# Hybrid decoder trunk on one core: expert steps of two 512-column blocks, 4 KB weight runs, later rows gathered from split operands

## The chip, the cores and the metric

The kernel runs on one core of one Trainium2 chip. The metric is the device time of one execution in microseconds (us). Before the change it is 1590.65 us, the median of 3 runs (1590.27 to 1591.75).

## What is computed

The reference runs two layers over a float32 residual stream of 256 tokens by 1024 features. Each layer has three token mixers (S5, SSD, gated DeltaNet) between an input and an output projection, and then a feed-forward part: dense SwiGLU in layer 0, and in layer 1 the top 2 of 8 SwiGLU experts, followed by a final RMSNorm. The change touches the experts alone:

```python
def moe_ffn(h, w_router, w_gate, w_up, w_down):
    logits = (h @ w_router).astype(jnp.float32)
    top_v, top_i = lax.top_k(logits, TOP_K)
    top_w = jax.nn.softmax(top_v, axis=-1)
    combine = jnp.sum(jax.nn.one_hot(top_i, N_EXPERTS) * top_w[..., None], axis=-2)
    out = jnp.zeros_like(h)
    for e in range(N_EXPERTS):
        out = out + combine[..., e:e + 1] * swiglu(h, w_gate[e], w_up[e], w_down[e])
    return out
```

`w_gate` and `w_up` are 1024 by 3584 for each expert and `w_down` is 3584 by 1024, all float32. That is 44.04 MB an expert and 352.3 MB for the eight, and every byte is read once.

## The kernel before

`moe` (L1326) does not multiply all 256 tokens by all experts. `route` finds for each token its two experts and its rank among the expert's tokens. From the ranks `one_hot` (L1387) builds 0/1 matrices, and `gather` (L1394) multiplies X by them on TensorE, which picks the rows of one expert into a few columns. Experts 2 to 6 have 64 slots, experts 0 and 1 have 64 and another 32 ("few"), expert 7 has 128 and 32. The rows are gathered in three batches (`BATCHES`, L1317): 64 columns for expert 2, 256 columns for experts 7 and 0, 352 columns for 3, 4, 5, 6 and 1. Batch 0 is gathered ahead of the branch (L1454 to L1455), the other two in pieces called `gap()` between the steps (L1673 to L1683). If any expert has more tokens than slots, a general path is taken (L1797 to L1800); with this data it is the other path, `stream` (L1669).

`stream` walks `STEPS` (L1313): 56 steps, each one expert and one block m of 512 of its 3584 inner columns. Experts 2 and 0 are interleaved first, then expert 7 with 3, 4 and 5, then 1 and 6. A step multiplies the gathered rows by the gate and up block (`half_up` L1522 for 64 slots with a gate and an up product side by side in the array; `few_up` L1530; `split_up` L1495 for expert 7), scales the result out of PSUM on ScalarE (L1735), then does the down product of the step before (`down` L1685, with `half_down`, `few_down`, `split_down`), and then turns its own gate and up result by TensorE transposes (`turn_half` L1558) and applies SiLU and the product (`gated` L1550). float32 matmuls show as two instructions each. Expert 7 alone works in float32r: `staged` (L1487) splits each weight tile into a high and a low part, by a ScalarE copy (L1491) and a VectorE subtraction (L1492), into buffers of which there are three. When an expert is done, `put_back` (L1641) adds its rows to X in two halves. These halves are called one at a time inside the next step's up product (L1729), as `late`.

TensorE's order is the order of the program (`manual_schedule`, L1803); the other engines' order is planned by the framework. PSUM has four banks of tag "G" for everything that is short-lived: up products, transposes, gathers and put-backs.

Weights come through a ring of 14 slots of 1 MB, loaded in the order of use by SyncE's queue. `load_up` (L1331) fills a slot with 256 rows of one gate block and one up block in two DMAs of 512 KB; a row of a block is a run of 2 KB in memory. `load_down` (L1341) fills one with 256 rows of `w_down`, two whole rows or 8 KB for each partition. A slot is loaded again when its last reader on TensorE is done. The first 14 loads are issued ahead of the branch (L1450).

Of the kernel before, what the change touches and what calls it, by code (L numbers as in the profile page):

```python
# [46 lines left out]
def tile_hymba_trunk(ctx: ExitStack, tc: tile.TileContext, p: dict, out: bass.AP):  # L47
# [1264 lines left out]
    BESIDE = [(e, m) for e in (3, 4, 5) for m in range(7)]  # L1312
    STEPS = [(2, 0), (2, 1), (2, 2), (0, 0), (0, 1), (2, 3), (0, 2), (0, 3), (2, 4), (0, 4), (2, 5), (0, 5), (2, 6), (0, 6)]  # L1313
    STEPS += [x for m in range(7) for x in BESIDE[3 * m:3 * m + 1] + [(7, m)] + BESIDE[3 * m + 1:3 * m + 3]]
    STEPS += [(1, 0), (6, 0), (1, 1), (6, 1), (1, 2), (1, 3), (6, 2), (1, 4), (6, 3), (1, 5), (6, 4), (1, 6), (6, 5), (6, 6)]

# [9 lines left out]
    def moe(ring):  # L1326
# [4 lines left out]
        def load_up(e, m, k2):  # L1331
# [23 lines left out]
        def ups(e, m):  # L1355
            return [lambda k2=k2: load_up(e, m, k2) for k2 in range(4)]

        def downs(e, m):
            return [lambda i=i: load_down(e, i) for i in (2 * m, 2 * m + 1)]

        def w_loads(steps):

            out, prev = [], None
            for x in steps:
                out += ups(*x) + (downs(*prev) if prev else [])
                prev = x
            return out + downs(*prev)
# [45 lines left out]
        def take_in(b, on=G, **kw):  # L1413

            c0, c1 = BOUNDS[b]
            oh = act.tile([128, 2, c1 - c0], F32, name="oh", **kw)
# [4 lines left out]
            def step(k):  # L1421
                if k == 7:
                    for e, first in BATCHES[b]:

                        o, n = PLACE[e, first]
                        slot_scale(rsl[:max(64, n), RS[e, first]:RS[e, first] + 1], oh[:, :, o - c0:o - c0 + n])
                px = ps("G", "pxe")[:, :c1 - c0]
                gather(px, k, oh, X)
# [19 lines left out]

        with scope("nrm"):
            ready = [f() for f in w_loads(STEPS)[:len(ring)]]  # L1450
            rest = route(cw, rk, cnt, r)
            todo = take_in(0, V)
            rest()
            for f in todo:  # L1454
                f()  # L1455

        with scope("experts"):
            def back(e, first=0):
# [4 lines left out]
                def rest():  # L1463
                    if e == STEPS[-1][0]:
                        slot_scale(cws, od, cw[:, :, e:e + 1])
                    ots[e, first] = turned(od, tag="ohT", bufs=5)
                return rest

            def more(e, n, x, x0, first=128):
# [3 lines left out]
                for k in range(8):  # L1473
                    px = ps("G", "pxm", (128, n))
                    gather(px, k, oh[:, :, :n], x0)
# [3 lines left out]
                return x, turned(oh, tag="ohT", bufs=5), rs  # L1479

            def wide_up(pgu, x, w, k2):
                for q in range(2):
                    for kk in range(2):
                        k = 2 * k2 + kk
                        T.matmul(pgu[q], lhsT=x[:, k], rhs=w[:, 2 * q + kk, :], start=k == 0, stop=k == 7)
# [8 lines left out]

            def split_up(pgu, w, k2):  # L1495
                for q in range(2):
                    h, l = staged(w[:, 2 * q:2 * q + 2])
# [24 lines left out]
            def half_up(pp, x, w, k2):  # L1522

                for kk in range(2):
                    k = 2 * k2 + kk
                    for q in range(2):
                        T.matmul(pp[64 * q:64 * q + 64], lhsT=x[:, k, :], rhs=w[:, 2 * q + kk, :], start=k == 0, stop=k == 7,  # L1527
                                 tile_position=(0, 64 * q), skip_group_check=True)

            def few_up(pp, x, w, k2):  # L1530

                for j in range(4):
                    T.matmul(pp[32 * j:32 * j + 32], lhsT=x[:, 2 * k2 + j % 2, :], rhs=w[:, j, :], start=k2 == 0, stop=k2 == 3,  # L1533
# [30 lines left out]
            def turn_few(g):  # L1564
# [5 lines left out]
                t = act.tile([128, 8 * FEW], F32, name="tf", tag="tf")  # L1570
# [3 lines left out]
                return gated(t, FEW, "hf")  # L1574
# [35 lines left out]
            def final(src, wF):  # L1610

                ss = act.tile([128, 2, 2], F32, name="ssf")
                for n in range(2):
                    for f in range(2):
                        j = act.tile([128, 512], F32, name="sqj", tag="gsf")
# [53 lines left out]
            def stream(ready):  # L1669
# [3 lines left out]
                two, one = (take_in(b, tag="y", bufs=3) for b in (1, 2))  # L1673
                todo = [lambda i=i: [f() for f in two[i:i + 2]] for i in range(0, 8, 2)] + one
# [6 lines left out]
                def gap():  # L1681
                    if todo:
                        todo.pop(0)()  # L1683

                def down(e, m, hs):  # L1685
                    split_ = GROUPS[e][0][1] == 128
                    if m == 0:
# [6 lines left out]
                    w = [take(), take()]  # L1694
                    for c2 in range(2):
                        (split_down if split_ else half_down)(acc[e][0], hs[0], w[c2], c2, m)
                    if len(hs) > 1:
                        for c2 in range(2):
                            few_down(acc[e][1], hs[1], w[c2], c2, m)
                    if (e, m) == STEPS[-1]:  # L1700
# [8 lines left out]
                    elif m == 6:  # L1709
                        assert not todo  # L1710
                        of = [(a, ots[e, first]) for a, (first, _) in zip(acc[e], GROUPS[e])]
                        late.extend(put_back(e, of[0], of[1:]) if split_ else put_back(e, None, of))

                for e, m in STEPS:
                    split_, few = GROUPS[e][0][1] == 128, len(GROUPS[e]) > 1
                    rs = [rsl[:, RS[e, first]:RS[e, first] + 1] for first, _ in GROUPS[e]]
                    pgu = [ps("G", "pmg") for _ in range(1 + split_)]
                    pgf = ps("G", "pmf") if few else None
                    for k4 in range(2):
                        w = [take(), take()]  # L1720
                        for k2 in range(2):
                            if split_:
                                split_up(pgu, w[k2], 2 * k4 + k2)
                            else:
                                half_up(pgu[0], rows(e, 0), w[k2], 2 * k4 + k2)
                        if few:
                            for k2 in range(2):
                                few_up(pgf, rows(e, GROUPS[e][1][0]), w[k2], 2 * k4 + k2)
                        if late:  # L1729
                            late.pop(0)()  # L1730
                    if split_:
                        g = gate(pgu, rs[0], "gs0")
                    else:
                        g = act.tile([128, 512], F32, name="gs", tag="gs0")
                        A.activation(out=g, in_=pgu[0], func=AF.Identity, scale=rs[0])  # L1735
                    if few:
                        gf = act.tile([128, 512], F32, name="gs", tag="gsf")
                        V.tensor_scalar(out=gf, in0=pgf, scalar1=rs[1], scalar2=None, op0=OP.mult)  # L1738
                    gap()
                    if prev:  # L1740
                        down(*prev)
                    gap()
# [3 lines left out]
                    if 2 <= m < 2 + len(GROUPS[e]):  # L1746
                        turns[e] = back(e, GROUPS[e][m - 2][0])
# [119 lines left out]
```

## Time and profile before

| | us |
|---|---|
| median of 3 runs | 1590.65 (1590.27 to 1591.75) |
| the profiled execution | 1594.89 |
| its span, first to last instruction | 1592.8 |
| before the experts' weights arrive | about 661 |
| expert stage, to the end of the last down product | about 661 to 1579 |

A profile is one execution. Busy TensorE time is the time between a matmul's start and its modelled end, so that a busy engine is not one at its peak; a "granted clock" of 1.00 is 2.4 GHz and 0.50 is 1.2 GHz. A "chain" is found by going back from the last instruction to what released it. "issue" is time in which nothing is seen that the engine waited for. GB/s is what the 16 DMA engines moved.

### The profile page before, as it was taken

The page shows a single profiled execution, that of the slowest core. Times are in us where ns is not written, and L with a number is a line of the kernel's source. Part 1 is how long each engine was busy: PE and PEld are TensorE (multiplying, and loading weights), DVE is VectorE, ACT ScalarE, POOL GpSimd, SP SyncE. Part 2 cuts the span into 40 slices and gives each one's busy share as a digit, 9 for nine tenths or more (in the row PEclk, how much of TensorE's full clock was granted, in tenths as well). Part 3 has the DMA queues.
Part 4 walks back from the last instruction along what each step waited for, and adds up shares of the span by engine and source line. Part 5 has one row for each costly group of instructions (what it writes and reads, how often), then busy time and mean ns, then how long its engine had stood idle before and what let it go on. Part 6 is the DMA issues. An engine that isn't in the chain of part 4 may idle for free.

```text
span 1592.8 us, 23174 instructions
## 1 busy us (share of the span) xinstructions
PE 1510.6 (95%) x9287; PEld 950.9 (60%) x9287; DVE 678.0 (43%) x1344; ACT 481.3 (30%) x817; POOL 156.9 (10%) x278
## 2 busy tenths in 40 slices
PE   4899979999999999889999999999999999999996
PEld 4898959999998999754333344544444444333322
DVE  7898684545567988520010051422422433100102
ACT  4562354454345543321110031321321332000101
POOL 5911081020000100030000000000000000000000
PEclk9999999999999989979999999999999999999998
DMA  6431044555545430399999999999999999999995
GB/s 171 146 105 53 1 149 132 186 182 177 189 156 146 133 107 1 116 360 381 356 348 396 398 395 398 395 398 396 398 396 398 397 397 397 398 397 395 398 397 203
DMA packets 203908, 435.80 MB, mean 274 GB/s; under 512 B 14539, under 2 KB 67876, under 8 KB 189712
## 3 DMA queue, kind: packets, MB, share of 16 engines
q1 hardware_dynamic: 201088, 432.20, 73.7%
q0 software_dynamic: 928, 1.43, 0.4%
q8 instruction: 75, 1.23, 0.3%
q10 hardware_dynamic: 1776, 0.60, 0.1%
q14 instruction: 41, 0.34, 0.1%
HBM read 433.15 MB, written 1.05 MB: 273 GB/s over the span
## 4 chain that ended last, share of the span: by engine, by line
PE 58%; DMA 7%; DVE 2%; ACT 1%; issue 1%; SPq 0%; DVEq 0%; ACTq 0%
PE pmg L1527 19%; PE macc L1587 10%; PE pmf L1533 5%; PE pmg L1501 4%; DMA ringb<-in_moe_w_down_dram 3%; PE maccf L1593 2%; PE macc L1510 2%; PE pmts L1561 2%; PE psc L1651 1%; DMA ringb<-in_moe_w_up_dram 1%; DMA ringb<-in_moe_w_gate_dram 1%; PE pxe L1396 1%; PE pl L789 1%; PE pd L798 1%; DVE los L1492 1%; DMA ringa<-in_moe_w_down_dram 1%
## 5 line engine op out<-in xcount | busy, mean ns | idle before, releaser
L1527 PE MATMUL pmg<-ringb,xs 128*64 128x512 f32 x1024 | 234.4, 601 | 4.3 <-issue 4.0
L216 DVE TENSOR_TENSOR wlo<-raw,whi 128x1024 fp32r<-128x1024 f32 (+3 forms) x109 | 180.3, 1656 | 103.3 <-ACT whi L215 103.1
L215 ACT ACTIVATE whi<-raw 128x1024 fp32r<-128x1024 f32 (+3 forms) x110 | 148.1, 1355 | 187.2 <-issue 80.7
L1527 PEld LDWEIGHTS pmg<-ringb,xs 128*64 128x64 f32 x1024 | 70.5, 137 | 137.2 <-issue 121.3
L1735 ACT ACTIVATE gs<-pmg,rsl 128x512 f32<-128x512 f32 x49 | 33.7, 687 | 345.0 <-PE pmg L1527 345.0
L1527 PE MATMUL pmg<-ringa,xs 128*64 128x512 f32 x544 | 123.5, 596 | 0.0
L1587 PE MATMUL macc<-ringb,hs 128*64 128x512 f32 x496 | 113.8, 597 | 2.3 <-DMA ringb<-in_moe_w_down_dram 2.3
L1555 DVE TENSOR_TENSOR hs<-hs,pmts 128x256 f32<-128x256 f32 x49 | 20.4, 417 | 220.5 <-ACT hs L1554 220.3
L1492 DVE TENSOR_TENSOR los<-ringb,his 128x1024 fp32r<-128x1024 f32 x54 | 63.6, 1220 | 69.7 <-ACT his L1491 55.1
L1391 POOL TENSOR_SCALAR od<-iota_f,rkk 128x128 f32<-128x128 f32 x22 | 15.5, 718 | 730.1 <-PE ptoh L1402 573.2
L1527 PEld LDWEIGHTS pmg<-ringa,xs 128*64 128x64 f32 x544 | 37.3, 137 | 73.7 <-issue 65.6
L1587 PEld LDWEIGHTS macc<-ringb,hs 128*64 128x64 f32 x496 | 33.8, 137 | 76.0 <-issue 69.4
L1738 DVE TENSOR_SCALAR gs<-pmf,rsl 128x512 f32<-128x512 f32 x21 | 15.8, 751 | 146.5 <-PE pmf L1533 146.5
L221 PE MATMUL pfg<-hT_hi,whi 128*128 128x256 f32 x224 | 63.5, 283 | 9.4 <-DVE xr_t L231 9.4
L1587 PE MATMUL macc<-ringa,hs 128*64 128x512 f32 x288 | 66.1, 596 | 0.0
L223 PE MATMUL pfu<-hT_hi,wlo 128*128 128x256 f32 x224 | 63.3, 283 | 0.9 <-DVE wlo L216 0.9
L1501 PE MATMUL pmg<-his,xw 128*128 128x512 f32 x224 | 63.1, 403 | 0.1
L223 PE MATMUL pfg<-hT_hi,wlo 128*128 128x256 f32 x224 | 63.1, 282 | 0.0
L222 PE MATMUL pfg<-hT_lo,whi 128*128 128x256 f32 x224 | 63.1, 282 | 0.0
L221 PE MATMUL pfu<-hT_hi,whi 128*128 128x256 f32 x224 | 63.1, 282 | 0.0
L222 PE MATMUL pfu<-hT_lo,whi 128*128 128x256 f32 x224 | 63.1, 282 | 0.0
L1554 ACT ACTIVATE hs<-pmts 128x256 f32<-128x256 f32 x49 | 18.8, 384 | 143.1 <-PE pmts L1561 142.0
(626 smaller groups left out, 2992.3 us busy)
## 6 DMA issues: line engine op xcount, KB each, us to landing
ringb<-in_moe_w_gate_dram SPq DMA_DIRECT2D x146, 512.0 KB, 13.0
ringb<-in_moe_w_up_dram SPq DMA_DIRECT2D x146, 512.0 KB, 11.4
ringb<-in_moe_w_down_dram SPq DMA_DIRECT2D x70, 1024.0 KB, 11.9
ringa<-in_moe_w_down_dram SPq DMA_DIRECT2D x40, 1024.0 KB, 11.9
ringa<-in_moe_w_gate_dram SPq DMA_DIRECT2D x78, 512.0 KB, 12.2
ringa<-in_moe_w_up_dram SPq DMA_DIRECT2D x78, 512.0 KB, 11.3
raw<-in_w_in_dram SPq DMA_DIRECT2D x16, 1024.0 KB, 5.9
raw<-in_ff_w_gate_dram SPq DMA_DIRECT2D x14, 1024.0 KB, 5.1
```

Of the source, the lines that this page charges most:

```text
L215: A.activation(out=h, in_=src, func=AF.Copy)
L216: on.tensor_tensor(out=l, in0=src, in1=h.bitcast(F32), op=OP.subtract)
L221: T.matmul(o, lhsT=lh, rhs=rh, start=start, stop=False)
L222: T.matmul(o, lhsT=lh, rhs=rl, start=False, stop=False)
L223: T.matmul(o, lhsT=ll, rhs=rh, start=False, stop=stop)
L1492: V.tensor_tensor(out=l, in0=src, in1=h.bitcast(F32), op=OP.subtract)
L1501: T.matmul(pgu[q], lhsT=xw[:, k, xo:xo + 128], rhs=part[:, kk], start=k == 0 and xo == 0 and part is h, stop=k == 7 and part is l)
L1510: T.matmul(acc[f], lhsT=h2[:, q, c * 128:c * 128 + 128], rhs=part[:, f * 512:f * 512 + 512], start=m + c + q == 0 and part is h, stop=m == ...
L1527: T.matmul(pp[64 * q:64 * q + 64], lhsT=x[:, k, :], rhs=w[:, 2 * q + kk, :], start=k == 0, stop=k == 7, tile_position=(0, 64 * q), skip_gr ...
L1533: T.matmul(pp[32 * j:32 * j + 32], lhsT=x[:, 2 * k2 + j % 2, :], rhs=w[:, j, :], start=k2 == 0, stop=k2 == 3, tile_position=(0, 32 * j), s ...
L1587: T.matmul(acc[64 * f:64 * f + 64], lhsT=h[:, c, :], rhs=w[:, cc, f * 512:f * 512 + 512], start=m == 0 and c == 0, stop=m == 6 and c == 3, ...
L1735: A.activation(out=g, in_=pgu[0], func=AF.Identity, scale=rs[0])
```

## The change

- Steps of experts 0 to 6 take two blocks (0 and 1, 2 and 3, 4 and 5) and then block 6 alone; expert 7 keeps one block a step. The order of the experts stays much the same. There are 35 steps where there were 56.
- `load_up` for two blocks takes 128 rows of 1024 columns of gate and up, so that a run is 4 KB. Loads of a single block (all of expert 7, block 6 of the others) keep 2 KB. A slot is 1 MB and a DMA 512 KB as before.
- In a step, all up products of both blocks come first, then the down products of both blocks of the step before, then all put-backs (`late`) that were open, then a group of gathers, then the turns of both blocks.
- The gathers of batches 1 and 2 use a float32r one-hot matrix and X split by `staged` into high and low parts: four float32r matmuls for each k of 128 features, in place of two float32 ones. They come in four groups (all 8 k of batch 1; 3, 3 and 2 k of batch 2), not twelve.
- The matmuls of the first gather move behind the branch; its one-hot matrix is still made ahead of it.
- Some buffers get other tags (`tf` uses the tile it turned, `ohT` has 4 buffers and not 5).

```diff
+    TWO = [(0, 1), (2, 3), (4, 5), (6,)]
+    BESIDE = [(e, ms) for e in (3, 4, 5) for ms in TWO]
+    STEPS = [(e, ms) for ms in TWO for e in (2, 0)]
+    for i_, x_ in enumerate(BESIDE):
+        STEPS += [x_] + [(7, (m_,)) for m_, at_ in enumerate((0, 1, 2, 4, 5, 6, 8)) if at_ == i_]
+    STEPS += [((1, 6)[j_ == '6'], TWO[i_]) for j_, i_ in zip('16161166', (0, 0, 1, 1, 2, 3, 2, 3))]
...
-            v = slot[:, :2048].rearrange("p (k n) -> p k n", k=4)
+            two = len(ms)
+            v = slot[:, :2048].rearrange("p (q k n) -> p q k n", q=2, n=512 * two)
             for q, w in enumerate((wg, wu)):
-                nc.sync.dma_start(v[:, 2 * q:2 * q + 2], w[e][256 * k2:256 * k2 + 256, m * 512:m * 512 + 512]
+                nc.sync.dma_start(v[:, q], w[e][256 // two * j:256 // two * (j + 1), ms[0] * 512:ms[0] * 512 + 512 * two]
...
         def gather(px, k, oh, src):
-            for n in range(2):
-                T.matmul(px, lhsT=src[:, n, k * 128:k * 128 + 128], rhs=oh[:, n, :], start=n == 0, stop=n == 1)
+            for i, x in enumerate(src):
+                for n in range(2):
+                    T.matmul(px, lhsT=x[:, n, k * 128:k * 128 + 128], rhs=oh[:, n, :], start=i + n == 0, stop=i + n == len(src))
...
-            todo = take_in(0, V)
+            first = with_moe(lambda: take_in(0, V))
             rest()
-            for f in todo:
-                f()
...
+            def split_x(k):
+                h, l = staged(X[:, :, 128 * k:128 * k + 512])
+                return [h, l]
...
-                two, one = (take_in(b, tag="y", bufs=3) for b in (1, 2))
-                todo = [lambda i=i: [f() for f in two[i:i + 2]] for i in range(0, 8, 2)] + one
+                for f in first:
+                    f()
+                todo = [take_in(b, parts=split_x, tag="y", bufs=3) for b in (1, 2)]
+                todo = [todo[0]] + [todo[1][i:i + 3] for i in (0, 3, 6)]
...
+                for e, ms in STEPS:
+                    gs = up(e, ms)
                     if prev:
+                        n_late = len(late)
                         down(*prev)
+                        for f in late[:n_late]:
+                            f()
+                        del late[:n_late]
+                    if todo:
+                        for f in todo.pop(0):
+                            f()
...
+                    hs = []
+                    for i, (g, gf) in enumerate(gs):
+                        hs.append([turn_split(g) if GROUPS[e][0][1] == 128 else turn_half(g, f"hs{i}")])
+                        if gf is not None:
+                            hs[-1].append(turn_few(gf, f"hf{i}"))
```

## Rows read from the trace of the kernel before

**Rows 1.** The profile's page: GB/s in 40 equal slices of the span.
```profile
GB/s 171 146 105 53 1 149 132 186 182 177 189 156 146 133 107 1 116 360 381 356 348 396 398 395 398 395 398 396 398 396 398 397 397 397 398 397 395 398 397 203
```

**Rows 2.** Stretches: length, busy PE, PEld, DVE, ACT, POOL; PE clock, DMA share, GB/s.
```profile
700.80:934.00 233.20, 233.19 (x1258) 84.87 (x1259) 28.05 (x59) 33.87 (x79) 12.50 (x23) 0.99 0.99 373
934.00:1342.00 408.00, 396.76 (x1931) 188.40 (x1931) 134.71 (x158) 115.34 (x150) 7.14 (x10) 1.00 1.04 397
1342.00:1512.00 170.00, 170.00 (x916) 56.98 (x914) 23.26 (x48) 16.54 (x36) 1.41 (x2) 1.00 1.04 397
```

**Rows 3.** The chain that ended last: start us, length us, what; single-block steps.
```profile
974.64 7.02 PE pmg L1527 x32
981.66 3.43 PE macc L1587 x16
985.10 0.68 PE pmts L1561 x4
985.77 7.02 PE pmg L1527 x32
```

**Rows 4.** The same chain, the first steps, where the gathers lie.
```profile
700.81 8.95 PE pmg L1527 x32
...
799.52 3.58 PE pmg L1527 x16
...
814.66 0.48 PE pmtf L1567 x4
815.14 3.58 PE pmg L1527 x16
...
832.78 7.02 PE pmg L1527 x32
...
845.76 3.58 PE pmg L1527 x16
...
861.54 7.02 PE pmg L1527 x32
```

**Rows 5.** TensorE's waits from 1342 to 1575 us: total, times, longest.
```profile
PE macc L1587 <- DMA ringb<-in_moe_w_down_dram: 2.3, 4, 0.7
PE pmg L1527 <- DMA ringb<-in_moe_w_up_dram: 0.3, 1, 0.3
```

**Rows 6.** Stretches: one amid gate and up loads, one amid the dense layer's down loads.
```profile
1455.50:1459.50 4.00, 4.00 (x20) 1.29 (x18) 0.00 (x0) 0.69 (x1) 0.00 (x0) 1.00 1.05 387
...
286.50:288.00 1.50, 1.50 (x15) 1.50 (x14) 0.41 (x1) 1.50 (x2) 0.00 (x0) 1.00 1.00 410
```

**Rows 7.** Timeline around the casts of a down product of expert 7.
```profile
1023.96 0.69 ACT L1735 ACTIVATE gs<-pmg,rsl 128x512 f32<-128x512 f32 x1 [5.33 <-PE pmg L1527]
1024.55 3.89 ACT L1491 ACTIVATE his<-ringa 128x1024 fp32r<-128x1024 f32 x4
1025.63 4.63 DVE L1492 TENSOR_TENSOR los<-ringa,his 128x1024 fp32r<-128x1024 f32 x4 [6.67 <-ACT his L1491]
1025.65 1.20 PE L1510 MATMUL macc<-his,ht 128*128 128x512 f32 x4 [1.73 <-ACT his L1491]
```

**Rows 8.** The sequencers at the branch: durations ns min/median/max, first and last start us.
```profile
L1797 PEldq COMPARE_BRANCH  x1: 6040/6040/6040, 694.6 to 694.6; - x1
...
L1795 POOLq TENSOR_LOAD <-cnt x1: 489/489/489, 689.8 to 689.8; - x1
```

**Rows 9.** Timeline: TensorE around the first gather.
```profile
688.96 6.24 PE L1396 MATMUL pxe<-oh,X 128*128 128x64 f32 x28
...
700.81 8.95 PE L1527 MATMUL pmg<-ringb,xs 128*64 128x512 f32 x32 [4.05 <-issue]
```

**Rows 10.** The chain again: 24 float32r matmuls of 512 columns.
```profile
934.27 5.59 PE pmg L1501 x24
```

**Rows 11.** Timeline: one evacuation of a gather of batch 1.
```profile
712.59 0.37 ACT L1432 ACTIVATE xw<-pxe,par 128x128 fp32r<-128x128 f32 x1 [0.32 <-PE pxe L1396]
```

**Rows 12.** The line that adds to X: count, duration ns min/median/max, first and last start.
```profile
L1598 DVE SCALAR_TENSOR_TENSOR X<-psc,cw,X x28: 741/750/753, 923.0 to 1567.4; 128x512 f32<-128x512 f32 x28
```

More of the change, by code (lines that the diff above doesn't have):

```diff
@@ L1353, in load_down @@
             return v
[L1355 to L1359, printed above, removed]
         def w_loads(steps):
[L1363 to L1367, printed above, removed]
+            out, prev = [], []
+            for e, ms in list(steps) + [(0, ())]:
+                out += [lambda e=e, ms=ms, j=j: load_up(e, ms, j) for j in range(4 * len(ms))]
+                out += prev
+                prev = [lambda e=e, i=i: load_down(e, i) for m in ms for i in (2 * m, 2 * m + 1)]
+            return out
         def of_block(g, c):
@@ L1447, in slot_scale, with with_moe @@
             A.activation(out=o, in_=pr, func=AF.Copy)
+        pmoe = cur['p']
+        def with_moe(f):
+            with using(pmoe):
+                return f()
         with scope("nrm"):
@@ L1715, in stream @@
                     split_, few = GROUPS[e][0][1] == 128, len(GROUPS[e]) > 1
-                    rs = [rsl[:, RS[e, first]:RS[e, first] + 1] for first, _ in GROUPS[e]]
-                    pgu = [ps("G", "pmg") for _ in range(1 + split_)]
-                    pgf = ps("G", "pmf") if few else None
+                    rs = [rsl[:, RS[e, f]:RS[e, f] + 1] for f, _ in GROUPS[e]]
+                    pgu = [ps("G", "pmg") for _ in range(1 + split_) for _ in ms]
+                    pgf = [ps("G", "pmf") for _ in ms] if few else None
@@ L1722, in stream @@
                             if split_:
-                                split_up(pgu, w[k2], 2 * k4 + k2)
+                                split_up(pgu, v, k2)
                             else:
-                                half_up(pgu[0], rows(e, 0), w[k2], 2 * k4 + k2)
-                        if few:
[L1727 to L1739, printed above, removed]
+                                for kk in range(2):
+                                    for i in range(len(ms)):
+                                        half_up(pgu[i], rows(e, 0), w[i][kk], 2 * k2 + kk)
@@ new lines, in up @@
+                            if few and (len(ms) == 2 or k2 % 2):
+                                for i, x in enumerate(wf):
+                                    if len(ms) == 2:
+                                        few_up(pgf[i], rows(e, GROUPS[e][1][0]), x, k2)
+                                    else:
+                                        few_up(pgf[0], rows(e, GROUPS[e][1][0]), x, k2 - 1 + i)
+                    out = []
+                    for i in range(len(ms)):
+                        if split_:
+                            g = gate(pgu, rs[0], "gs0")
+                        else:
+                            g = act.tile([128, 512], F32, name="gs", tag=f"gs{i}")
+                            A.activation(out=g, in_=pgu[i], func=AF.Identity, scale=rs[0])
+                        gf = None
+                        if few:
+                            gf = act.tile([128, 512], F32, name="gs", tag=f"gf{i}")
+                            V.tensor_scalar(out=gf, in0=pgf[i], scalar1=rs[1], scalar2=None, op0=OP.mult)
+                        out.append((g, gf))
@@ L1749, in stream @@
+                    prev = (e, ms, hs)
+                assert not late
                 cur['wF'] = norm_weight()
@@ L1759, in expert @@
                 acc = [[ps("PS"[t], f"macc{t}{f}") for f in range(2)] for t in range(nt)]
-                rest = w_loads([(e, m) for m in range(7)])
+                rest = w_loads([(e, (m,)) for m in range(7)])
                 def take():
```

92 lines of the change are left out of this document (47 added, 45 removed).

## The prediction

> **What bounds the kernel now.** I read the page first, for where the bytes move: from slice 18 on the DMA engines move 350 to 398 GB/s to the end [rows 1]. So the expert stage, about 900 us of 1592.8, looks bound by weights. The view by stretches then sets TensorE beside the DMA engines [rows 2]. In the first stretch (experts 2 and 0) TensorE is busy all the time and the transfers run at 373 GB/s; in the next two they run at 397 GB/s with the DMA engines' share at 1.04, which is full, while TensorE is still busy 97 to 100%. Both are near their limit. The chain of work decides between them: for most of the stage it is TensorE's own instructions back to back. A step of one block and 64 slots is an up product of 7.02 us, a down product of 3.43 and a turn of 0.68, and the next step starts 11.13 us after the first, with nothing between [rows 3]. TensorE waits for a weight transfer only at the end: 2.6 us in all after 1342 us [rows 5]. So TensorE's instruction stream sets the end, the ring's lead of 14 slots is eaten up slowly, and transfers set the pace for the last tens of microseconds alone. A change is worth what it takes out of TensorE's stream, and faster transfers are worth those 2.6 us, plus the room that a shorter stream needs.
>
> **The sum** is made against the profiled execution: its span is 1592.8 us, its own time 1594.89, and the median of the runs 1590.65, 4.2 lower. I subtract the sum from the median.
>
> *Turns.* No matmul of an expert goes away: two blocks have the same 64 up and 32 down instructions. What goes is the change between kinds. A turn of 0.68 us holds four transposes. A second group of four right behind the first, as the few-slot turn is today, takes 0.48 [rows 4]. The first up product behind a turn takes 7.02 us for 32 instructions, where 16 of the same size take 3.43, so 0.16 more [rows 3]. One turn less is 0.20 + 0.16 = 0.36 us. Seven experts merge three pairs each: 21 x 0.36 = 7.6. For experts 0 and 1 a few-slot product now stands ahead of a second down product, 0.15 more for each of six pairs, so -6.7 us. Ends: 0, if each saved start is only paid elsewhere, and -7.6.
>
> *Gathers.* The first six steps take 799.52 - 700.81 = 98.7 us [rows 4]. The same kinds of step without gathers take 7.70 (an up product and a turn, 7.02 + 0.68), 11.13 twice [rows 3], 15.78 (845.76 to 861.54), 17.64 (815.14 to 832.78) and 12.98 (832.78 to 845.76) [rows 4], 76.4 together. Of the 22.3 left, 1.9 is the first up product, 8.95 against 7.02 us. So batches 1 and 2 cost 20.4 us now. After the change each has 32 matmuls in float32r. One of 512 columns takes 5.59 / 24 = 0.233 us [rows 10], so by columns 0.117 for 256 and 0.16 for 352: 3.7 + 5.1 us. Four groups with a start of 0.36 each add 1.5, the row scales that stay about 1. Batch 1 is evacuated by two ScalarE operations of 0.37 us for each k [rows 11], 0.74 against 4 x 0.117 = 0.47 on TensorE, and eight in a row now wait for it: 7 x 0.27 = 1.9. That is 13.2, so -7.2 us. X must be split four times, 0.97 on ScalarE (3.89 for four) and 1.16 on VectorE (4.63 for four) [rows 7]. I cost it at nothing, since ScalarE has only the scalings to do during the down product ahead; with that cover gone each is 2.1 us, 8.5 in all. Ends: +1.3 and -9.1 (no wait for evacuation).
>
> *Transfers.* Amid loads in 2 KB runs the rate is 387 GB/s; amid the dense layer's down weights, 4 KB runs, it is 410 when the engines are full [rows 6]. The mean of 397 [rows 2] with two thirds of the bytes in 2 KB and a third in 8 KB runs puts 8 KB at 419. Of 352.3 MB, 176.2 now go in 4 KB runs (six sevenths of gate and up of seven experts), 58.7 stay at 2 KB, 117.4 at 8 KB: 152 + 430 + 280 = 862 us at 410 against 887. The 25 us move no end by themselves. They take away the 2.6 us of waits and keep up with a stream that is shorter by some 14 us. So -2.6; ends: 0, if 4 KB runs go at 387, and -5, if weight loads waited too. The Trainium skill (DMA: Bandwidth & Descriptors, section Specifications) has runs of 512 B or more at line rate, by which 4 KB would gain nothing over 2 KB. The trace disagrees, with 387 and 410 GB/s [rows 6]. The same page (section iDMA fabric) gives 408.7 GB/s for a stream in 4 KiB rows, by which the sum of the transfers would be 863 us.
>
> *First gather.* It now stands behind the branch. TensorE's branch took 6.04 us, from 694.6, and ran beside the gather, which ended at 696.76, 4.05 ahead of the first up product [rows 8, 9]. The count it needs was there by 689.8, when GpSimd read it in 0.49 us [rows 8]. After the change TensorE reads the count at about 689.8, branches from 690.3 to 696.3, gathers for 7.8 (688.96 to 696.76) and starts the experts at 704.1, not 700.8: +3.3 us. Ends: +1.4, if the slow first up product (1.9 us) is over by then, and +7, if it comes later in full. SyncE's loads ahead of the branch don't move.
>
> *Casts of expert 7.* Its down product waited 1.73 us for a cast that stood on ScalarE behind the scaling of the up product before, 0.69 us [rows 7]. Behind a step of two blocks there are two scalings. Five of seven down products get one more: 5 x 0.69 = +3.5. Ends: 0, if the cast is planned ahead of the scalings, and +20 (first rival).
>
> *Put-backs.* All four products of an expert now stand together, and each is added to X by a VectorE operation of 0.75 us [rows 12], 3.0 us for a bank after bank, where TensorE needs 4 x 2 x 0.233 = 1.9. The turn behind them needs those banks. I take 0.3 us for each of seven experts, +2; ends 0 and +5.
>
> Down products, few-slot products, ScalarE's and VectorE's own totals stay, and lie beside TensorE. SyncE issues the same number of DMAs, 512 KB each. **Sum:** -6.7 - 7.2 - 2.6 + 3.3 + 3.5 + 2.0 = -7.7 us, so 1583 us.
>
> **Rivals.**
> *ScalarE's order holds up expert 7 (slower).* Up and down products of expert 7 live on casts, of which only three fit ahead, and ScalarE runs in order. If casts are queued behind both scalings and both SiLUs of a two-block step, and those SiLUs wait for TensorE's turns, then each of seven steps loses a cast and its subtraction at the up product as well, 0.97 + 1.16 = 2.1, and 0.7 more at the down product: 20 us instead of 3.5, and 1583 + 16 = 1599. It decides against the change from about 1.6 us of new wait a step. For it: the wait is there today [rows 7]. Against: only the down product has it; the up product that I looked at starts right behind its turn. Chance 0.11.
> *Transfers stay the limit.* If 4 KB runs go at 387 GB/s, the transfers still need 887 us. They run fuller at the start, where TensorE held the ring back (373 against 397 GB/s [rows 2]), and TensorE would wait some 7 us at the end instead of 2.6: about -4, 1587. Against: rows 6. Chance 0.10.
> *More than I count.* If the first up product runs at full pace, the casts are planned well and put-backs cost nothing, the terms are -7.6 - 9.1 - 2.6 + 1.4 = -18: 1573. Chance 0.13.
> *It doesn't do what it says.* Splitting X, the evacuations and the branch eat the gathers' saving, and merged turns wait for PSUM banks: near 1590. Chance 0.06.
> The forecast itself has 0.60.
>
> **How the numbers follow.** A measurement of this kernel tells 0.2%, 3.2 us, from no change, so faster means under 1587.5 and slower over 1593.8. From the forecast I count 0.54 as faster and 0.06 within; from the transfers' case 0.05 and 0.05; the larger gain, 0.13, is faster; the last case, 0.06, is within; of ScalarE's case 0.02 is within and 0.09 slower. That is 0.72, 0.19 and 0.09. The range goes from 1573, the larger gain, to 1591, past the transfers' case and the last one; it leaves out ScalarE's case and some of the far side of the larger gain.
>
> **What would show it.** A two-block step of 64 slots should take 21.9 us from up product to up product, not 22.3; the gathers' instructions should be float32r at about 0.12 and 0.16 us each, 13 us with their waits. Stretches amid two-block up loads should move 405 GB/s or more, and no wait of TensorE for a transfer should be left after 1342 us. The first up product should start near 704. TensorE's wait for a cast at L1510's line should be near 2.4 us where it was 1.7. It would be wrong if TensorE shows waits for casts at the up product of expert 7, if a step begins with TensorE waiting for a PSUM bank, or if the stage still ends with waits for transfers.

## The result, and the profile after

The changed kernel takes 1572.74 us (median of 4 runs, 1572.53 to 1576.38), the kernel before 1590.6 beside it (4 runs): ratio 0.9892, interval [0.9875, 0.9909]. That is 17.9 us where I forecast 7.7, and 0.3 us under the range's low end.

The spans differ by more, 1592.8 to 1571.0. The profiled execution before had one stretch at a low granted clock, in a layer mixer that the change doesn't touch, and the one after had it not. The stretch 561 to 572 us, before and then after (columns as in [rows 2]):

```profile
561.00:572.00 11.00, 11.00 (x52) 11.00 (x52) 9.02 (x32) 4.69 (x9) 0.00 (x0) 0.53 0.45 171
```
```profile
561.00:572.00 11.00, 10.57 (x86) 10.57 (x87) 10.97 (x35) 4.69 (x9) 0.00 (x0) 1.00 0.58 192
```

86 matmuls lie in it at clock 1.00 and 52 at 0.53. So I compare the expert stage alone: from the end of routing's last matmul to the end of TensorE's last instruction it takes 892.4 us before (688.9 to 1581.3) and 873.5 after (686.0 to 1559.5). The change gained 18.9 there.

The page after, GB/s in 40 slices, as [rows 1], and the stretches of [rows 2]:

```profile
GB/s 172 148 108 54 1 133 126 188 161 193 186 172 145 146 127 2 61 320 340 405 413 406 406 407 408 388 393 407 408 401 396 406 411 408 411 414 411 408 404 203
```
```profile
700.80:934.00 233.20, 230.63 (x1296) 84.89 (x1296) 27.07 (x59) 36.06 (x83) 8.58 (x14) 0.99 0.98 386
934.00:1342.00 408.00, 397.67 (x1964) 191.55 (x1965) 141.89 (x167) 117.71 (x151) 7.07 (x10) 1.00 1.02 403
1342.00:1512.00 170.00, 169.64 (x954) 55.83 (x952) 19.58 (x45) 15.37 (x33) 1.41 (x2) 1.00 1.02 411
```

In the last two stretches the transfers go at 403 and 411 GB/s where they went at 397, with the DMA engines as full as before (a share of 1.02, where it was 1.04). TensorE is as busy as before. Both got shorter by about the same: by the landing times in the traces, the last weight lands 884.9 us after the end of routing before and 864.5 after, 20.4 less, and TensorE's stage is 18.9 shorter.

Lines have moved: L1527 is now L1538 (up), L1587 is L1598 (down), L1561 is L1572 (turn), L1651 is L1662 and L1598 is L1609 (put-back), L1510 is L1523 and L1491 is L1499 (expert 7's down product, casts), L1735 is L1757 (scaling).

The chain after: the first up product and gather, pieces of two-block steps, and the end (compare [rows 3, 4]):

```profile
701.60 15.83 PE pmg L1538 x64
717.43 1.64 PE pxe L1396 x12
...
820.36 13.88 PE pmg L1538 x64
...
845.34 0.96 PE pmts L1572 x8
...
868.05 7.02 PE macc L1598 x32
...
1510.71 12.62 DMA ringb<-in_moe_w_down_dram
...
1528.80 15.30 DMA ringa<-in_moe_w_down_dram
```

An up product, a down product and a turn of two blocks with 64 slots are 13.9 + 7.02 + 0.96 = 21.9 us, as forecast. At the end the chain goes through two weight loads: TensorE got there so early that a transfer released it.

TensorE's waits from 690 us on (total, times, longest; compare [rows 5]):

```profile
PE macc L1523 <- ACT his L1499: 8.8, 5, 1.8
PE pxe L1396 <- issue: 7.9, 1, 7.9
PE macc L1598 <- DMA ringa<-in_moe_w_down_dram: 1.6, 3, 0.6
PE pmts L1572 <- DVE X L1609: 1.5, 3, 0.6
PE macc L1598 <- DMA ringb<-in_moe_w_down_dram: 1.0, 2, 0.7
```

Casts for expert 7 (L1499), the branch, and still 2.6 us for weights at the end. Waits for X before a turn (L1572) are new.

### The profile page after: what moved, and what is told of

The parts are those of the page before. It is cut to its first block, busy times and chain, and to the rows that moved or that the text cites. A ratio compares the mean times of both kernels' runs of the same rounds, so it can differ in the third digit from the quotient of the medians.

```text
span 1571.0 us, 23148 instructions
## 1 busy us (share of the span) xinstructions
PE 1481.2 (94%) x9287; PEld 941.5 (60%) x9287; DVE 682.4 (43%) x1348; ACT 486.4 (31%) x821; POOL 160.6 (10%) x278
## 2 busy tenths in 40 slices
DMA packets 160901, 435.81 MB, mean 277 GB/s; under 512 B 14539, under 2 KB 67876, under 8 KB 146704
## 4 chain that ended last, share of the span: by engine, by line
PE 60%; DMA 5%; DVE 2%; ACT 1%; issue 1%; DVEq 0%; ACTq 0%; SPq 0%
PE pmg L1538 19%; PE macc L1598 10%; PE pmg L1514 5%; PE pmf L1544 5%; PE macc L1523 2%; PE maccf L1604 2%; DMA ringb<-in_moe_w_down_dram 2%; PE pmts L1572 2%; PE pxe L1396 1%; DMA ringa<-in_moe_w_down_dram 1%; PE pl L789 1%; PE pd L798 1%; PE psc L1662 1%; DMA ringa<-in_moe_w_gate_dram 1%; DMA ringb<-in_moe_w_gate_dram 1%
## 5 line engine op out<-in xcount | busy, mean ns | idle before, releaser
L1538 PE MATMUL pmg<-ringb,xs 128*64 128x512 f32 x976 | 220.7, 600 | 0.0
L1538 PEld LDWEIGHTS pmg<-ringb,xs 128*64 128x64 f32 x976 | 67.6, 138 | 134.8 <-issue 122.7
L1757 ACT ACTIVATE gs<-pmg,rsl 128x512 f32<-128x512 f32 x49 | 33.7, 687 | 336.3 <-PE pmg L1538 334.3
L1538 PE MATMUL pmg<-ringa,xs 128*64 128x512 f32 x592 | 132.2, 594 | 0.0
L1500 DVE TENSOR_TENSOR los<-ringb,his 128x1024 fp32r<-128x1024 f32 x64 | 75.8, 1222 | 107.5 <-ACT his L1499 107.5
L1598 PE MATMUL macc<-ringb,hs 128*64 128x512 f32 x504 | 113.8, 595 | 1.0 <-DMA ringb<-in_moe_w_down_dram 1.0
L1538 PEld LDWEIGHTS pmg<-ringa,xs 128*64 128x64 f32 x592 | 41.5, 137 | 83.2 <-issue 77.3
L1598 PEld LDWEIGHTS macc<-ringb,hs 128*64 128x64 f32 x504 | 34.8, 137 | 77.5 <-issue 73.1
L1499 ACT ACTIVATE his<-ringb 128x1024 fp32r<-128x1024 f32 x64 | 65.7, 1055 | 20.7 <-PE pmg L1514 18.2
L1598 PE MATMUL macc<-ringa,hs 128*64 128x512 f32 x280 | 63.6, 596 | 1.6 <-DMA ringa<-in_moe_w_down_dram 1.6
```

What stands on the lines that cost most here:

```text
L1499: A.activation(out=h, in_=src, func=AF.Copy)
L1500: V.tensor_tensor(out=l, in0=src, in1=h.bitcast(F32), op=OP.subtract)
L1538: T.matmul(pp[64 * q:64 * q + 64], lhsT=x[:, k, :], rhs=w[q], start=k == 0, stop=k == 7, tile_position=(0, 64 * q), skip_group_check=True)
L1598: T.matmul(acc[64 * f:64 * f + 64], lhsT=h[:, c, :], rhs=w[:, cc, f * 512:f * 512 + 512], start=m == 0 and c == 0, stop=m == 6 and c == 3, ...
L1757: A.activation(out=g, in_=pgu[i], func=AF.Identity, scale=rs[0])
```

## The experiments

Most are read with one table that I worked out from the traces. The time from the end of one TensorE instruction to the end of the next, waits included, is put down to the later one's group, and each group is summed over the stage named above (us; columns are the runs that follow):

```
                  before  b_few  b_cast  after  a_few  2k     apart  cast1  c1_few both2
up, 64 slots      354.8   352.8  360.8   345.8  345.8  361.6  345.8  353.6  346.6  355.0
down, 64 slots    176.0   172.8  181.1   175.3  171.6  179.6  172.2  179.8  173.7  179.4
turns             48.4    48.5   48.4    48.4   48.4   48.5   44.7   48.4   48.7   48.4
expert 7          137.0   136.9  126.1   134.0  133.1  134.0  134.9  121.7  121.0  121.7
gathers           29.8    29.8   29.8    31.2   31.3   31.4   31.2   31.2   31.2   23.5
put-backs         23.6    23.6   23.6    16.0   16.1   16.1   22.4   16.1   16.1   16.1
few slots, last   122.8   122.8  122.8   122.9  122.8  122.8  122.9  122.9  122.9  122.9
whole stage       892.4   887.1  892.6   873.5  869.0  894.0  874.0  873.5  860.0  866.8
```

(b_few is before_fewer_held, b_cast before_cast_first, a_few after_fewer, 2k runs_2k, apart late_apart, cast1 cast_first, c1_few cast_first_fewer, both2 both_again. The branch's idle time stands in "up" before, and with the gathers after.) Several medians below lie within each other's intervals; differences of a few us are read from the stage, which came out at 892.4 and 892.9 us in two profiles of the kernel before and at 873.5 and 873.4 in two of the changed kernel.

**Runs of 2 KB in the changed kernel.** Same slots and bytes, same instructions on TensorE. The columns of a row still lie side by side in memory; the slot's layout cuts each row into two pieces of 2 KB, which brings the DMA packets back from 160901 to 203908, the number of the kernel before.

```diff
+            if two == 2:
+                v = slot[:, :2048].rearrange("p (i q n) -> p q i n", i=2, q=2)
+                for q, w in enumerate((wg, wu)):
+                    nc.sync.dma_start(v[:, q], w[e][128 * j:128 * j + 128, ms[0] * 512:ms[0] * 512 + 1024]
+                                      .rearrange("p (i n) -> p i n", i=2))
+                return v
...
```

> The kernel after, with the same 512 KB transfers of two blocks cut into runs of 2 KB (a slot holds gate and up of one block, then of the other). Theory: the transfers fall back to about 397 GB/s and need some 25 us more in all, TensorE hides most of it, and waits for transfers at the end grow to 10 us or more, since TensorE's stream is 19 us shorter than before: 1577 to 1584. Rival (4 KB runs gained nothing beyond the 2.6 us of waits): 1573 to 1575. The rate amid up loads should be 385 to 390 GB/s where it is 405 to 411 after.

1596.3 us, ratio 1.0018 [0.9998, 1.0038]: all of the gain is gone. The stretches of this run:

```profile
934.00:1342.00 408.00, 396.58 (x1962) 191.38 (x1958) 144.64 (x171) 119.08 (x153) 7.04 (x10) 1.00 1.04 397
1342.00:1512.00 170.00, 165.08 (x872) 52.86 (x870) 17.45 (x40) 14.61 (x30) 1.41 (x2) 1.00 1.04 397
```

397 GB/s again, and TensorE, as short in its own work as after the change, idles in the second of them and waits for weights from 1342 us on:

```profile
PE macc L1604 <- DMA ringb<-in_moe_w_down_dram: 2.9, 5, 0.7
PE macc L1604 <- DMA ringa<-in_moe_w_down_dram: 2.7, 5, 0.7
PE pmg L1544 <- DMA ringa<-in_moe_w_up_dram: 1.7, 6, 0.3
PE pmg L1544 <- DMA ringb<-in_moe_w_up_dram: 1.1, 4, 0.3
```

The list has 8.4 us; the table has 15.7 more for up products and 4.3 for down products than after the change. The rest is not idle time: idle stretches of 0.15 us or less, which the list leaves out, add up to 0.2 us in these products. It is time in which TensorE runs one instruction where it otherwise runs two or more: by the starts and ends in the trace, a single one is under way for 14.1 us of the 64-slot products, where the changed kernel has 1.2. A timeline of this run:

```profile
1448.22 1.07 PE L1544 MATMUL pmg<-ringa,xs 128*64 128x512 f32 x2
1449.57 2.43 PE L1544 MATMUL pmg<-ringa,xs 128*64 128x512 f32 x8 [0.28 <-DMA ringa<-in_moe_w_up_dram]
1452.28 1.08 PE L1544 MATMUL pmg<-ringa,xs 128*64 128x512 f32 x4 [0.28 <-DMA ringa<-in_moe_w_up_dram]
```

The gate block has landed and the up block not, so the two instructions of a gate product run by themselves, and then TensorE stands. Ten instructions take 4.06 us, from 1448.22 to 1452.28, where the chain after has 13.88 / 64 = 0.22 us for each, 2.2 in all; the list has 0.56 of the 1.9 lost.

I had expected that TensorE would hide most of it. The Trainium skill (DMA: Bandwidth & Descriptors, section Specifications) has line rate from 512 B on; here 2 KB against 4 KB runs are 20.5 us of the stage.

**One block a step in the changed kernel**, gathers, first gather and put-backs as changed (which takes 2 KB runs with it).

```diff
-    STEPS = [(e, ms) for ms in TWO for e in (2, 0)]
...
+    STEPS = [(e, (m,)) for e, m in STEPS]
...
-                    at = ms[0] // (1 if e == 7 else 2) - 1
+                    at = ms[0] - 2
```

> The kernel after, but every step has one block, in the order of the kernel before, so that all gate and up runs are 2 KB; gathers, put-backs and the first gather stay as after. Theory: the 21 turns saved cost 7 us again, and the transfers, back at 397 GB/s, add waits at the end: 1580 to 1586. Rival (steps of two blocks bring nothing but 4 KB runs): as the kernel with 2 KB runs. Rival (most of the gain is in the merged steps): 1588 or more.

1592.31 us, ratio 0.9993 [0.9976, 1.001]. Nothing, though I had expected half of the gain to stay. The run takes away merged steps and 4 KB runs together and can't price the steps by themselves: runs_2k, which keeps the merged steps, had lost everything as well.

**Put-backs together, in the kernel before**, after the down product:

```diff
-                        if late:
-                            late.pop(0)()
...
+                        n_late = len(late)
                         down(*prev)
+                        for f in late[:n_late]:
+                            f()
+                        del late[:n_late]
```

> The kernel before with one part of the change: both halves of an expert's put-backs stand together behind the down product, with nothing else moved. Theory (pairs): put-backs fall from 23.6 to about 16 us on TensorE, and the kernel gains 5 to 8 us, less what its transfers, which end level with TensorE in this kernel, give back: 1584 to 1587, with more waits for transfers near the end than 2.6 us. Rival (fewer starts): 2 to 3 us, 1588.

1594.36 us, ratio 1.0013 [0.9995, 1.0031], though its put-backs take 16.1 us where they took 23.6. Counted as in the table, the 7.5 us are spent elsewhere on TensorE: expert 7's products take 142.4 us where they took 137.0, and turns 50.2 where they took 48.4. 3.5 us of waits for X stand on its list ahead of turns and up products, and the list before has none there. So TensorE's work as a whole was not shorter in this run.

**Put-backs apart, in the changed kernel**, one half ahead of the down product and one behind it:

```diff
+                        if n_late:
+                            late.pop(0)()
                         down(*prev)
-                        for f in late[:n_late]:
-                            f()
-                        del late[:n_late]
+                        if n_late:
+                            late.pop(0)()
```

> The kernel after, but an expert's two halves of put-backs stand apart again, one ahead of the down products and one behind them. Theory (pairs): put-backs fell from 23.6 to 16.0 us of TensorE's time because the products of the two halves lie on different 64 rows of the array and run two at a time once they stand together; apart they take 0.23 us each again, so 5 to 7 us come back: 1578 to 1580. Rival (fewer starts): only the second start and return of each group is paid again, 7 times 0.36: 2 to 3 us, 1575. Rival (transfers set the gain): no more than 1 us.

1574.71 us, ratio 0.9892 [0.9859, 0.9924], the same as the change, and not the 1578 or more that I expected of the pairs. The table shows why: put-backs +6.4, but turns -3.7, since none waits for X, and down products -3.1, since its list has no waits for weights. Timelines of put-backs, after the change and then in this run:

```profile
1116.07 1.21 PE L1662 MATMUL psc<-y,ohT 64*128 64x512 f32 x8
```
```profile
1107.95 1.20 PE L1662 MATMUL psc<-y,ohT 64*128 64x512 f32 x4
...
1116.09 1.19 PE L1662 MATMUL psc<-y,ohT 64*128 64x512 f32 x4
```

Eight products of 64 rows (float32r, so each is one instruction) take the time of four. The first half's rows are at the array's rows 0 to 63 and the second's at 64 to 127, and standing together they run two at a time. The Trainium skill (TensorE: Matmul & The Clock Gate, Part 3: Packing small matmuls) says that products of fewer than 128 rows at separate row positions overlap, and the trace agrees: 1.21 us for eight against 1.20 for four.

**First gather ahead of the branch again:**

```diff
             rest()
+            for f in first:
+                f()
...
```

> The kernel after, with the first gather's products ahead of the branch again, as before. Theory: TensorE's branch of 6 us runs beside the gather again, so 3 to 4 us are gained: 1569 to 1570, which beats the kernel after. Rival: the first products start no earlier, because ScalarE or the clock holds them: 1572 to 1573.

1571.09 us, ratio 0.9848 [0.9825, 0.9871]. The stage takes 870.6, 3.0 less: this move costs about what I forecast (3.3), and here it comes through, for TensorE frees the first slots earlier: the first load into a slot that an expert's product has freed is issued 15.6 us after routing's end where it was 19.3, and the last weight lands 3.0 us earlier.

**Gathers in float32** (`take_in(b, tag="y", bufs=3)`, without `parts=split_x`):

> The kernel after, with batches 1 and 2 gathered from X in float32 again, in the same four groups; no split of X. Theory: 64 products of 0.22 and 0.30 us in place of 64 of 0.12 and 0.16: gathers cost 6 to 7.5 us more of TensorE's time, less 2 that were waits for evacuation: 1577 to 1580. Rival (the gain was in the fewer groups): 1574.

1579.39 us, ratio 0.9903 [0.9881, 0.9925]. The products of the gathers (L1396) take 6.0 us more in the trace, and the stage 3.3 more (876.8); the waits for weights fall from 2.6 to 1.5 us and give some of it back.

**Casts for expert 7's down product ahead of the scalings:**

```diff
...
+                    if prev and prev[0] == 7:
+                        wd_ = [take(), take()]
+                        held.append((wd_, [staged(wd_[0][:, c:c + 1]) for c in range(2)]))
...
+                            with ExitStack() as st:
+                                if held:
+                                    st.enter_context(tc.issue_after(cur['cast'].ins))
+                                A.activation(out=g, in_=pgu[i], func=AF.Identity, scale=rs[0])
```

> The kernel after, with the first two casts of expert 7's down product put ahead of the scalings of the up product before it in ScalarE's order. TensorE waits about 1.8 us for the first cast in five of seven down products after. Theory: these waits go, and the scalings behind the casts are hidden by the down product: 8 to 9 us gained in TensorE's stream; the transfers, which have some 10 us of lead, keep up or give back a part: 1564 to 1568. Rival: the weights to cast have not landed by then, and ScalarE holds the turn up instead: 1572 or slower.

1574.13 us, ratio 0.9866 [0.9832, 0.9899]. TensorE takes 12.3 us less for expert 7's products, and 7.7 more for up and 4.5 more for down products: 873.5, the same to a tenth, and the last weight lands at the same 864.5 us. I had expected 1564 to 1568. Its waits for weights:

```profile
PE macc L1598 <- DMA ringb<-in_moe_w_down_dram: 2.9, 5, 0.7
PE macc L1598 <- DMA ringa<-in_moe_w_down_dram: 2.7, 5, 0.7
```

So after the change the transfers are the limit. The next runs take 24 transfers out (`ms[0] > 0` in the changed kernel): the up matrix of expert 7 isn't loaded for blocks 1 to 6, and its products work on what lay in the slot. They are for timing only.

```diff
-            for q, w in enumerate((wg, wu)):
+            for q, w in enumerate((wg, wu)[:2 - (e == 7 and m > 0)]):
```

> The changed kernel, without the same 24 transfers (expert 7's up matrix of blocks 1 to 6 isn't loaded). Theory (after the change TensorE's stream and the transfers are level again): 2.6 us of waits at the end go, and under 1 us of small ones: about 1569.5, ratio 0.987. Rival (transfers are the bound after the change by a wide margin): 1565 or less. Rival (TensorE alone is the bound): 1572.7, no change.

1568.84 us, ratio 0.9859 [0.9832, 0.9886]: 4 us lower, stage 869.0, and no wait for weights is listed. That is TensorE's own length after the change.

> The changed kernel with the casts of expert 7's down product planned ahead of the scalings, without the same 24 transfers. Theory (the 12 us that TensorE no longer waits for casts were taken back by waits for transfers): with room in the transfers they come through: some 12 us below the changed kernel without these transfers, about 1557.5, ratio 0.979. Rival (casts planned earlier delay other work of ScalarE or VectorE by as much): equal to the changed kernel without these transfers, about 1569.5.

1561.16 us, ratio 0.98 [0.9776, 0.9824], stage 860.0. With room in the transfers, 9 of the casts' 12 us come through, and 1.4 us of listed waits for weights are back.

> The kernel before, without 24 of its transfers: the up matrix of expert 7 for blocks 1 to 6 isn't loaded (12.6 MB of 352 MB, some 31 us of transfer at 403 GB/s), and its products work on what lay in the slot; TensorE's instructions stay the same. Theory (TensorE's stream and the transfers were level in the kernel before): with the transfers made 31 us shorter, only TensorE's few waits for them go, 2.7 us at the end: about 1587, ratio 0.998. So 4 KB runs without a shorter TensorE stream would be worth no more than that. Rival (the transfers alone set the end before, and 4 KB runs gave the 18 us by themselves): 1573 or less, ratio 0.989 or below.

1573.07 us, ratio 0.9874 [0.985, 0.9898]: a miss, and at first sight the rival's number. But the framework plans ScalarE's order with the transfers, and planned it otherwise. The waits for casts (9.7 us before) are gone from this run, and expert 7's products take 120.4 us where they took 137.0; set beside the kernel before, all of the 16.4 us gained by 1360 us lie between its first and last step, and 5.2 behind 1500. So the run took out two things, and I repeated it with the first cast held behind the scaling:

```diff
...
+                    with ExitStack() as st:
+                        if m and c == 0:
+                            st.enter_context(tc.issue_after(cur['scaled'].ins))
...
-                        A.activation(out=g, in_=pgu[0], func=AF.Identity, scale=rs[0])
+                        cur['scaled'] = A.activation(out=g, in_=pgu[0], func=AF.Identity, scale=rs[0])
```

> The kernel before, without the 24 transfers of expert 7's up matrix (blocks 1 to 6, 12.6 MB; its products work on what lay in the slot), and with the cast for expert 7's down product held behind the scaling, as the kernel before has it. Theory (in the kernel before, TensorE waited for transfers only at the end, and the rest of what its run without these transfers gained came from the casts, which had moved ahead of the scalings): about 5 us from transfers after 1500 us, 1585.5, ratio 0.997. Rival (the transfers alone had set the end of the kernel before): 1573 to 1575, ratio 0.988. The prediction's own term, 2.6 us: 1588, ratio 0.998.

1589.56 us, ratio 0.9968 [0.9951, 0.9986]; stage 887.1, and no wait for weights is listed. Fewer transfers alone were worth 5.3 us of the stage in the kernel before, 2.8 by the medians (1592.38 beside it). The order isn't quite that of the kernel before: expert 7's products take the same in all, but its up products 3.1 us less and its down products 3.0 more.

And the casts alone in the kernel before (same edit as in cast_first, for its one scaling):

> The kernel before with all its transfers, with the casts for expert 7's down product ahead of the scaling. Theory (a shorter stream of TensorE is worth nothing while the transfers are in 2 KB runs): TensorE's 12 to 16 us at the casts come back as waits for transfers from 1342 us on: 1590, ratio 0.999 to 1.000. Rival (TensorE's stream alone set the end of the kernel before): 1576 to 1579, ratio 0.992.

1590.87 us, ratio 0.9992 [0.9977, 1.0006]. TensorE has 10.9 us less in expert 7, and 5.9 and 5.1 more in up and down products (b_cast in the table). Waits of this run:

```profile
PE macc L1587 <- DMA ringb<-in_moe_w_down_dram: 4.1, 7, 0.7
...
PE pmg L1527 <- DMA ringb<-in_moe_w_up_dram: 1.7, 4, 0.7
PE macc L1587 <- DMA ringa<-in_moe_w_down_dram: 1.6, 3, 0.6
```

**Both, gather ahead and casts first**, in the changed kernel, and once more beside it on one chip:

> The changed kernel with the first gather ahead of the branch again and the casts of expert 7's down product ahead of the scalings; all transfers as in the change. Theory (transfers are the limit in all of it from the first steps on): the gather ahead lets the first slots come free 3 us earlier, so 3 us of its own come through and the casts' 12 us don't: about 1569 to 1570, ratio 0.985 to 0.987. Rival (waits of TensorE add up as they stand): 1572.7 - 3 - 12 = 1557.5, ratio 0.979.

1568.42 us, ratio 0.9854 [0.9828, 0.9879], stage 868.3.

> The changed kernel, unchanged, on the same chip as the other runs of this set: 1572 to 1574, ratio 0.988 to 0.990.

1573.52 us, ratio 0.9879 [0.9856, 0.9902].

> The changed kernel with the first gather ahead of the branch and the casts of expert 7's down product ahead of the scalings, beside the changed kernel on the same chip. Theory (of both, only the gather's 3 us come through, since transfers are the limit): 3 to 4 us below the changed kernel, 1569 to 1570. Rival (the difference seen before lies between chips): equal.

1568.17 us, ratio 0.985 [0.9829, 0.987], stage 866.8 against 873.4 beside it. It is 5.3 us below the change in the medians, though the two intervals overlap, and the fastest version here that loads all weights. The gather alone had given 3.0; why the two together give 2 to 4 more (868.3 and 866.8) is open. A second profile of the kernel before (1597.82 us) had the low clock near 561 us as well, and a stage of 892.9; so had the second one of the changed kernel (1580.59 us, clock 0.57 there, stage 873.4). The low clock there is not the change's doing.

## Why the prediction was wrong

**What failed: two terms of the sum, both of the wrong sign.** With the transfers out of the way (b_few and a_few in the table) TensorE's own stage went from 887.1 to 869.0, -18.2; the prediction's terms for TensorE add up to -5.1. The stage's 18.9 is this 18.2, and the 5.3 us lost to late weights before, less the 4.5 lost after.

- *"Casts of expert 7. ... 5 x 0.69 = +3.5."* Measured -3.9 between b_few and a_few, -3.0 between the two kernels. The two scalings are not both late. Timeline of ScalarE and then TensorE after the change:

```profile
1024.22 0.69 ACT L1757 ACTIVATE gs<-pmg,rsl 128x512 f32<-128x512 f32 x1 [11.37 <-PE pmg L1538]
1025.08 0.69 ACT L1757 ACTIVATE gs<-pmg,rsl 128x512 f32<-128x512 f32 x1 [0.17 <-PE pmg L1538]
1025.66 3.89 ACT L1499 ACTIVATE his<-ringb 128x1024 fp32r<-128x1024 f32 x4
```
```profile
1017.54 7.46 PE L1538 MATMUL pmg<-ringa,xs 128*64 128x512 f32 x34
1026.76 1.20 PE L1523 MATMUL macc<-his,ht 128*128 128x512 f32 x4 [1.76 <-ACT his L1499]
```

The blocks of a step alternate in the up product, so block 0 is done 0.86 us ahead of block 1, and its scaling runs beside block 1's last matmuls. The wait is 1.76 us, as it was 1.73 [rows 7], and not 2.4. It comes in five of seven down products, where six had one. Two now stand behind a single-block step and have none: there ScalarE has two casts done ahead of the scaling. The first halves of expert 7's up products, 6.45 us in five of seven before, take 6.46 in one and 6.22 in another, else 5.84 to 5.92. Between the kernels these up products give 1.8 of the 3.0 us and the down products 1.2; between b_few and a_few the down products give 4.5 and the up products take 0.6 more. So the size depends on how the framework plans ScalarE's order; both pairs show a gain, and not the loss that I forecast.

- *"Put-backs. ... I take 0.3 us for each of seven experts, +2."* Measured -3.9: 7.5 less for the products that now run in pairs, 3.7 more in turns that wait for X. I had priced the wait and not looked at which rows of the array the products use.

**What held.** *Turns*, -6.7: up products -3.0 (without the branch's 4.05), turns -3.7 (as late_apart has them), together -6.7; down products gave 1.2 more. *Gathers* and *first gather*, -7.2 + 3.3 = -3.9: measured -2.5, of which the branch's idle time grew from 4.05 to 7.85 us and the rest fell by 6.3 (14.1 us with waits, where I had 13.2). *The rate*: 403 and 411 GB/s over the two long stretches, where the sum's 352.3 MB in 862 us make 409; the last weight lands 20.4 us earlier, where I had 25. The first up product started at 701.60 and not at 704 only because routing ended 2.9 us earlier in that execution; from routing's end it is 15.6 us against 11.9. The float32r gathers wait little for ScalarE (0.7 us listed at the products, 0.7 at the row sums). Casts, put-backs, down products and gathers make up the 13.1 us: 7.4 + 5.9 + 1.2 - 1.4.

**What was half right.** *"TensorE's instruction stream sets the end"* and *"The 25 us move no end by themselves"*: taken alone, fewer transfers were worth only 5.3 us (before_fewer_held), the 2.6 us on the list and as much that is not on it. But a shorter stream alone was worth nothing in the three runs that had one (one_block, runs_2k, before_cast_first). The landing times say the same: after routing's end the last weight lands at 884.9 us in the kernel before, at 885.1 in before_cast_first and at 884.9 in runs_2k, however long TensorE's own work is, and TensorE ends 7.5 to 9.1 us behind it; in before_fewer_held, where TensorE leads, it ends 18.0 us behind it. So the transfers set the end before, by 5 us: the two were nearly level, 887 and 892, and I read from 2.6 us of waits that TensorE led. I did write that the transfers "keep up with a stream that is shorter"; that was the change's larger service, and I had it as a remark. The *-2.6* itself came to -0.7: 5.3 us lost to weights before, 4.5 after, because TensorE shortened by about as much as the transfers. The list of what would make the prediction wrong had this sign: the stage still ends with waits for transfers.

**The rivals.** *More than I count* gave 1573 and the time is 1572.7, by luck and not by its terms: it took the gathers at -9.1 and the branch at +1.4 (about -6.3 and +3.8), and casts and put-backs at nothing. *Transfers stay the limit* took 387 GB/s for 4 KB runs; runs_2k shows that this would have meant no gain at all, not 4 us. *ScalarE's order* is excluded by the waits for casts, 8.8 us in all. *It doesn't do what it says* fell with the result.

## What to carry to other kernels

Where an engine is 97 to 100% busy and the DMA engines are full beside it, both set the end: price a change on both, since the new end is the later of the two, and an edit that shortens one alone can measure as nothing (before_cast_first: 10.9 us less for expert 7, 0.2 us more for the stage). Find out each one's own length by leaving out work of the other (a few transfers, a cast's wait), with the planned order held, before any edit is sized; and see when the last weight lands: where that time stays while TensorE's work gets shorter, the transfers set the end. And when work is moved together, look at which rows of the array it uses and which instruction of the step ahead is really the last.

## What was unexpected in the hardware

- Two groups of four float32r products of 64 rows, on different halves of the array's rows, take 1.21 us together and 1.20 us each when they stand apart.
- 2 KB against 4 KB runs in half of the bytes: 397 against 403 to 411 GB/s over long stretches, in DMAs of the same 512 KB, and also where the 2 KB pieces lie side by side in memory (runs_2k).
- Late weights cost more than the list of waits has: runs_2k lists 5.8 us more than the changed kernel and its stage is 20.5 us longer. Much of the rest shows as busy time, in which a single instruction is under way (14.1 us, where the changed kernel has 1.2).
